# Dense expert tiles of a decoder trunk on one core: 64 early score chunks instead of 32, one copy for four tokens' gate products, gate steps given priority

## The chip, the core and the metric

The kernel runs on 1 core of one Trainium2 chip. The metric is the time of one execution on the device in microseconds (us). The engines are named as in the profile: PE is TensorE's matmuls, PEld its weight loads, DVE is VectorE, ACT is ScalarE, POOL is GpSimd, SP is SyncE, which here only issues transfers.

## What is computed

One layer of a decoder trunk, for a prompt of 1024 tokens and 32 sample tokens of width 1024. First come a modulation by a conditioning vector, one projection, three token mixers (a matrix memory, a gated unit, a pooling), an output projection and a layer norm. Then every token goes through a layer of 16384 small experts (PEER), and a second layer norm. The change concerns that expert layer. Cut to it:

```python
def peer(xm, w_pq, peer_keys, peer_u, peer_v):          # 8 heads, 128 keys, top 16
    q = jnp.einsum('nd,de->ne', x2, w_pq).reshape(n, PEER_HEADS, 2, PEER_DK)
    s = jnp.einsum('nhpd,hpkd->nhpk', q, peer_keys)
    s1, i1 = lax.top_k(s[:, :, 0], PEER_TOPK)
    s2, i2 = lax.top_k(s[:, :, 1], PEER_TOPK)
    cand = (s1[..., :, None] + s2[..., None, :])         # and cidx = i1 * 128 + i2
    top_s, top_pos = lax.top_k(cand, PEER_TOPK)
    idx = jnp.take_along_axis(cidx, top_pos, axis=-1)
    g = jax.nn.softmax(top_s, axis=-1)
    act = gelu(jnp.einsum('nd,nhkd->nhk', xk, peer_u[ik]))
    return jnp.einsum('nhk,nhkd->nd', gk * act, peer_v[ik])
```

So each token has 8 x 16 = 128 experts out of 16384, each with a row of `peer_u` and a row of `peer_v` (1024 numbers each).

## The kernel before

The prompt is cut into 8 tiles of 128 tokens; the 32 sample tokens are a ninth, small tile. The expert layer is done in two ways.

*Gathered tiles* (0, 1, 6, 7 and the small one): for each token slot one indirect transfer on GpSimd's queue fetches 128 rows of `peer_u` (0.524 MB), VectorE multiplies and sums them with the tokens; later 128 rows of `peer_v` come the same way and TensorE adds them up, two rows per four matmuls, into two PSUM banks (`acc`, L1354). Row buffers are few (6 of one kind and 6 of another), so a row is fetched when an older one has been used. There are 544 such steps for `peer_u` and 544 for `peer_v`; `g_gather` writes them, and gives their instructions a priority 2000 ahead of the place where they are written.

*Dense tiles* (2, 3, 4, 5, 512 tokens): all 16384 experts are computed for them, in 128 chunks of 128 experts. The score of a chunk (`scores`, L1067) is 24 matmuls of 128x128 by 128x512, since `peer_u` and the tokens are both split into a high and a low half-precision part; ScalarE and VectorE do the split of a loaded chunk of `peer_u`. The scores go through gelu, are multiplied by the gate of that token and expert (zero for the experts that are not chosen), split again, and four chunks at a time (a group) are multiplied with the split `peer_v` (`out`, L1174: 8 outputs of 12 matmuls for a group), whose sums VectorE adds up in SBUF (L1183). There are 32 groups. `g_dense` writes them; for each output it also writes a part of the next group's scores.

*The gates* of a dense tile (`g_weights`): for a token, a 128x128 table with a gate at (i1, i2) is a product of two matrices of ones and gates, with the gate in a high and a low part. VectorE makes the two masks for 16 tokens at a time (`ab`, L1042 and L1043), multiplies one by the high part (L1044), and gets the low part by a product for tokens NL to 15 (L1045), while ScalarE does it for tokens 0 to NL - 1 (L1047). TensorE makes two matmuls for each token (`pgm`, L1054), ScalarE copies four tokens' tables out of PSUM in two halves (L1057), turning them so that the token is the innermost index, into two tiles `gs` of 64 columns by 32 tokens. Every 32 tokens the two tiles are stored to DRAM (`G_d`, L1061). The dense stage loads them by group (L1105).

*Early scores* (`g_pre`): the scores of the chunks in `PRE`, one in four, are made before the dense stage: `peer_u` is loaded (0.524 MB), split (L1084 on ScalarE, L1085 on VectorE), the scores are copied (L1089) and stored to DRAM (`sd_d`, 0.262 MB, L1090). In the dense stage such a chunk's scores are loaded instead of its `peer_u` (L1143).

The order: the parts are generators. `run` books for each step three costs in us (TensorE, VectorE, transfers), always takes the part whose planned time is least, and so sets the order in which instructions are written. A scheduler then puts them into each engine's fixed order by their priority, which is the place of writing, less `AHEAD` for the parts named there: the mixing, routing and recurrence parts have 1000, the gate steps none. The main part waits until all gates, all early scores, the routing (`g_route`, `g_choice`) and 96 rows of tile 1's second gather are written, closes the early buffers and begins the dense stage. The costs booked in the dense stage are, for an output, an early chunk and any other chunk:

```python
            if op[0] == "o":
                yield 2.58, 0.66, 0
            elif op[1] in PRE:
                yield 0, 2.9, 3.0
            else:
                yield 5.15, 1.77 + 2.2, 3.7
```

and for a gathered row `c = 0, 1.14, 1.46` (`peer_u`) or `c = 0.43, 0, 1.46` (`peer_v`).

Of the kernel before, what the change touches and what calls it, by code (L numbers as in the profile page):

```python
# [7 lines left out]
F32 = mybir.dt.float32  # L8
# [5 lines left out]
AF = mybir.ActivationFunctionType  # L14
# [3 lines left out]
P = 128  # L18
# [10 lines left out]
LOW = -3.0e38  # L29
BUFS = {"ws": 5, "x": 2, "s": 6, "h": 8, "w": 3, "t": 4, D: 1, D // 2: 2}  # L30
LAG = 4
AHEAD = {"g_mixed": 1000, "g_routed": 1000, "g_even": 1000, "g_odd": 1000}
SPLIT = 1
COND = "ada", 0
EARLY = "proj", "gate"
# [18 lines left out]
ND = len(DENSE) * P  # L54
TB = 32
BB = 16
NL = 6
PRE = [4 * g + 3 for g in range(32)]
GROUP = 4
SW, SU, SV, SG_, SC = 2.0 ** 8, 2.0 ** 8, 2.0 ** 6, 2.0 ** 12, 0.25  # L60
CANDS = [(j, 16 // (j + 1)) for j in range(16)]
# [17 lines left out]
def kernel(ctx: ExitStack, tc: tile.TileContext, A, O):  # L79
    nc = tc.nc  # L80
    mm, tr = nc.tensor.matmul, nc.tensor.transpose
    V, S = nc.vector, nc.scalar
# [25 lines left out]
    def run(*parts):  # L108
# [6 lines left out]
        while parts:  # L115
# [8 lines left out]
            now = p[0]  # L124
            ahead = AHEAD.get(p[2].__name__, 0)
            tc.cur_priority -= ahead
# [44 lines left out]
    G_d = dram.tile([ND // TB, P, P, TB], F32, name="G_d")  # L171
    qkvo_d = dram.tile([NT + 1, P, 4, 512], F32, name="qkvo_d")
    sd_d = dram.tile([max(len(PRE), 1), P, ND], F32, name="sd_d")
    xd_d = dram.tile([len(DENSE), P, 2, KD, P], F16, name="xd_d")
# [840 lines left out]
    def g_weights(i, t):  # L1015

        sc = cur["build"]
# [18 lines left out]
        for b in range(P // BB):  # L1036
            ab = sc.tile("ab", [P, 3, BB, P], F16, 2)
            pairs = lambda a: a.rearrange("p t (c e) -> p t c e", e=2)
            f = [fx[:, j, b * BB:b * BB + BB, :].unsqueeze(2).to_broadcast([P, BB, P // 2, 2]) for j in range(4)]
            one = iota16.rearrange("p (c e) -> p c e", e=2).unsqueeze(1).to_broadcast([P, BB, P // 2, 2])  # L1040
            eq = ab[:, 2]
            V.tensor_tensor(out=pairs(ab[:, 0]), in0=one, in1=f[0], op=ALU.is_equal)  # L1042
            V.tensor_tensor(out=pairs(eq), in0=one, in1=f[1], op=ALU.is_equal)  # L1043
            V.tensor_tensor(out=pairs(ab[:, 1]), in0=pairs(eq), in1=f[2], op=ALU.mult)  # L1044
            V.tensor_tensor(out=pairs(eq[:, NL:]), in0=pairs(eq[:, NL:]), in1=f[3][:, NL:], op=ALU.mult)  # L1045
            for j in range(NL):
                S.activation(eq[:, j], eq[:, j], AF.Copy, scale=fl[:, b * BB + j:b * BB + j + 1])  # L1047
            if b * BB % TB == 0:
                gs = [sc.tile("gs", [P, 64, TB], F32, 2) for _ in range(2)]
            for t4 in range(0, BB, 4):  # L1050
                pg = bank("pgm", (P, 4, P))
                for j in range(4):
                    for e in range(2):
                        mm(pg[:, j, :], lhsT=ab[:, 0, t4 + j, :], rhs=ab[:, 1 + e, t4 + j, :], start=(e == 0), stop=(e == 1))  # L1054
                t0 = b * BB % TB + t4
                for e in range(2):
                    S.activation(gs[e][:, :, t0:t0 + 4].rearrange("p c t -> p t c"), pg[:, :, 64 * e:64 * e + 64], AF.Copy)  # L1057
                yield 0.6, 1.1, 0.4 * MB
            if (b + 1) * BB % TB == 0:
                for e in range(2):  # L1060
                    nc.sync.dma_start(G_d[i * (P // TB) + b * BB // TB, :, 64 * e:64 * e + 64, :], gs[e])  # L1061

    def scores(ps, us, xd):
        m = 0
# [5 lines left out]
    def g_pre():  # L1070
# [7 lines left out]
        for i in range(len(DENSE)):  # L1078
            nc.sync.dma_start(xd[:, i], xd_d[i])
        for i, n in enumerate(PRE):  # L1080
            u = xslab("up", (P, KD, P))
# [12 lines left out]
    def g_dense(sc):  # L1094
# [11 lines left out]

        todo = [n for n in range(nch) if n not in PRE]

# [31 lines left out]
        def ld_s(n):  # L1140
            if n in PRE:
                PS[n] = sc.tile("act", [P, ND], F32, 3)
                nc.sync.dma_start(PS[n], sd_d[PRE.index(n)])  # L1143

# [5 lines left out]
        def coef(n):  # L1150
            ps = PS.pop(n)
            if n in PRE:
                t = ps
# [572 lines left out]
```

## Time and profile before

| what | value |
|---|---|
| median of 3 runs | 3282.22 us (3278.94 to 3289.62) |
| the profiled execution, its own time | 3289.84 us |
| its span in the profile | 3288.1 us |
| PE busy | 2763.4 us, 84% |
| DVE busy | 2205.8 us, 67% |
| POOL busy | 1320.7 us, 40% |
| ACT busy | 938.7 us, 29% |
| transfers | 964.86 MB, mean 293 GB/s |

An engine's busy time is the sum over its instructions; a busy PE is not PE at its peak, because matmuls overlap and their ends are modelled. The clock column of the views is the granted TensorE clock as a share of full speed. The DMA column is the mean busy share of the core's 16 DMA engines. A "releaser" behind an idle time is what the engine waited for last.

### The profile page before, as it was taken

What the parts mean: (1) busy time and instruction counts of PE and PEld (TensorE: products, weight loads), DVE (VectorE), ACT (ScalarE), POOL (GpSimd) and SP (SyncE); (2) the same over time, 40 slices, a digit from 0 to 9 for tenths busy, and PEclk for the clock granted to TensorE, in tenths of its full rate; (3) what the DMA queues carried; (4) which work ended last, traced back from release to release, by engine and by line L of the source; (5) the groups of instructions that cost most, each with busy time, mean ns of one, the idle gap of its engine ahead of it and who ended that gap; (6) DMA issues with size and microseconds to landing.
All of it is one profiled execution on the core that took longest, in us unless ns stands there. A gap on an engine that the chain in (4) does not pass through costs nothing.

```text
span 3288.1 us, 44890 instructions
## 1 busy us (share of the span) xinstructions
PE 2763.4 (84%) x16366; PEld 1415.8 (43%) x16366; DVE 2205.8 (67%) x5763; ACT 938.7 (29%) x1618; POOL 1320.7 (40%) x1096
## 2 busy tenths in 40 slices
PE   6888983587976798987657999999999999559996
PEld 3447942444654356753333443344333343004443
DVE  2443998767788657789985774877777775015557
ACT  3413243112011124324564322322222222003331
POOL 0000366535444530045754454655665553650000
PEclk8988996688978899999867999999999999559998
DMA  9753898889998984488999999999999998993442
GB/s 293 253 175 132 300 347 296 293 294 327 322 341 275 336 324 155 161 318 308 346 356 361 333 353 348 379 374 364 385 387 353 345 382 291 333 325 123 144 126 76
DMA packets 370577, 964.86 MB, mean 293 GB/s; under 512 B 36933, under 2 KB 114884, under 8 KB 366252
## 3 DMA queue, kind: packets, MB, share of 16 engines
q0 software_dynamic: 156672, 570.49, 47.7%
q1 hardware_dynamic: 213684, 391.51, 34.2%
q8 instruction: 128, 2.10, 0.3%
q14 instruction: 93, 0.76, 0.1%
HBM read 892.92 MB, written 69.02 MB: 293 GB/s over the span
## 4 chain that ended last, share of the span: by engine, by line
PE 48%; DMA 12%; DVE 9%; issue 7%; ACT 2%; POOL 1%; SPq 0%; POOLq 0%; DVEq 0%; ACTq 0%
PE po L1174 19%; PE psd L1067 16%; DMA row<-in_peer_v,iT 6%; PE acc L1354 6%; DMA row<-in_peer_u,ii 3%; PE py L809 2%; DVE row L1297 2%; PE pqr L881 2%; POOL row L1270 1%; DMA G_d<-gs 1%; ACT gs L1057 1%; DMA v<-in_peer_v 1%; DMA act<-sd_d 0%; PE pvp L280 0%; DMA wo<-in_w_o 0%
## 5 line engine op out<-in xcount | busy, mean ns | idle before, releaser
L1270 POOL DMA_INDIRECT row<-in_peer_u,ii x544 | 679.8, 1250 | 987.2 <-DVE ii L1293 312.5
L1270 POOL DMA_INDIRECT row<-in_peer_v,iT x544 | 638.7, 1174 | 608.9 <-PE acc L1354 369.1
L1297 DVE SCALAR_TENSOR_TENSOR row<-row,x2u 128x1024 f32<-128x1024 f32 x544 | 657.2, 1215 | 161.9 <-DMA row<-in_peer_u,ii 148.7
L1067 PE MATMUL psd<-xd,us 128*128 128x512 f16 x3072 | 712.6, 384 | 21.1 <-ACT us L1084 15.0
L1174 PE MATMUL po<-vs,coef 128*128 128x512 f16 x3072 | 701.3, 381 | 19.9 <-ACT vs L1137 11.7
L1354 PE MATMUL acc<-row,cexp 128*32 128x512 f32 x2176 | 362.3, 720 | 176.4 <-DMA row<-in_peer_v,iT 175.5
L1174 PEld LDWEIGHTS <-coef 128*128 128x128 f16 x3072 | 294.5, 98 | 437.5 <-issue 81.3
L1067 PEld LDWEIGHTS <-us 128*128 128x128 f16 x3072 | 298.1, 99 | 418.5 <-issue 56.6
L881 PE MATMUL pqr<-x2T,wpq 128*128 128x128 f32 (+1 forms) x2304 | 282.2, 282 | 2.0 <-DVE z L817 1.0
L881 PEld LDWEIGHTS pqr<-x2T,wpq 128*128 128x128 f32 x2304 | 274.7, 198 | 8.9 <-DVE CA L929 1.5
L1159 DVE SCALAR_TENSOR_TENSOR act<-act,scale,g 128x512 f32<-128x512 f32 x128 | 95.9, 750 | 232.9 <-ACT act L1157 230.6
L1157 ACT ACTIVATE act<-psd,scale 128x512 f32<-128x512 f32 x96 | 65.9, 687 | 597.6 <-PE psd L1067 597.6
L1183 DVE SCALAR_TENSOR_TENSOR acc<-po,scale,acc 128x512 f32<-128x512 f32 x248 | 183.2, 746 | 71.0 <-PE po L1174 70.5
L1354 PEld LDWEIGHTS acc<-row,cexp 128*32 128x32 f32 x2176 | 49.9, 116 | 354.6 <-DMA row<-in_peer_v,iT 240.7
L1138 DVE SCALAR_TENSOR_TENSOR vs<-v,vs 128x1024 f16<-128x1024 f32 x128 | 155.5, 1219 | 47.0 <-ACT vs L1137 46.9
L1137 ACT ACTIVATE vs<-v 128x1024 f16<-128x1024 f32 x128 | 133.6, 1051 | 136.0 <-PE po L1174 68.0
L809 PE MATMUL py<-wo,Y 128*128 128x512 f32 (+1 forms) x288 | 141.5, 641 | 18.2 <-DMA wo<-in_w_o 11.5
L1054 PE MATMUL pgm<-ab 128*128 128x128 f16 x1024 | 100.9, 256 | 66.2 <-DVE ab L1044 30.4
L1057 ACT ACTIVATE gs<-pgm 128x256 f32<-128x256 f32 x256 | 124.9, 641 | 68.3 <-PE pgm L1054 42.6
L280 PEld LDWEIGHTS <-w 128*128 128x128 f16 x2160 | 124.0, 100 | 22.6 <-issue 19.5
L1121 DVE SCALAR_TENSOR_TENSOR us<-u,us 128x1024 f16<-128x1024 f32 x96 | 117.4, 1223 | 19.9 <-ACT us L1120 19.9
L1054 PEld LDWEIGHTS <-ab 128*128 128x128 f16 x1024 | 83.2, 118 | 102.3 <-issue 55.4
(344 smaller groups left out, 2860.0 us busy)
## 6 DMA issues: line engine op xcount, KB each, us to landing
v<-in_peer_v SPq DMA_DIRECT2D x128, 512.0 KB
u<-in_peer_uT SPq DMA_DIRECT2D x96, 512.0 KB
wpq<-in_w_pq SPq DMA_DIRECT2D x64, 512.0 KB
G_d<-gs SPq DMA_DIRECT2D x32, 1024.0 KB
g<-G_d SPq DMA_DIRECT2D x32, 1024.0 KB
wada<-in_w_ada SPq DMA_DIRECT2D x48, 512.0 KB
wf<-in_w_in SPq DMA_DIRECT2D x44, 512.0 KB
wo<-in_w_o SPq DMA_DIRECT2D x32, 512.0 KB
```

Source lines behind the costliest of these rows:

```text
L809: mm(py[t, e][:ns[t]], lhsT=Y_[t][:, k + j, :ns[t]], rhs=w[:, j, :], start=(k + j == 0), stop=(k + j == KD - 1))
L881: mm(pq[:, i * P:i * P + ns[t]], lhsT=w[:, k, :], rhs=X2[t][:, k, :ns[t]], start=(k == 0), stop=(k == KD - 1))
L1054: mm(pg[:, j, :], lhsT=ab[:, 0, t4 + j, :], rhs=ab[:, 1 + e, t4 + j, :], start=(e == 0), stop=(e == 1))
L1057: S.activation(gs[e][:, :, t0:t0 + 4].rearrange("p c t -> p t c"), pg[:, :, 64 * e:64 * e + 64], AF.Copy)
L1067: mm(ps, lhsT=us[a][:, k, :], rhs=xd[:, :, b, k, :], start=(m == 0), stop=(m == 23))
L1137: S.activation(vs[:, 0], v, AF.Copy, scale=SV)
L1138: V.scalar_tensor_tensor(out=vs[:, 1], in0=v, scalar=SV, in1=vs[:, 0], op0=ALU.mult, op1=ALU.subtract)
L1174: mm(po, lhsT=d[:, a, i * P:(i + 1) * P], rhs=vs[:, b, c % 2, :], start=(m == 0), stop=(m == 3 * GROUP - 1))
L1183: V.scalar_tensor_tensor(out=a, in0=po, scalar=scale[:, 3:4], in1=a, op0=ALU.mult, op1=ALU.add)
L1270: nc.gpsimd.indirect_dma_start(out=s[:], out_offset=None, in_=A[table], in_offset=bass.IndirectOffsetOnAxis(ap=idx, axis=0))
L1297: V.scalar_tensor_tensor(out=s, in0=s, scalar=1.0, in1=x2, op0=ALU.mult, op1=ALU.mult, accum_out=sv[:, k:k + 1])
L1354: return mm(pv[e][g:g + 32, :], lhsT=l, rhs=s[:, e * 512:e * 512 + 512], start=(j == 0), stop=(j == nj - 1), skip_group_check=True)
```

## The change

Four edits. `PRE` names every second chunk instead of every fourth, so 64 chunks' scores are made early and 64 are left for the dense stage. `NL` goes from 6 to 3, so ScalarE scales 3 of 16 tokens and VectorE 13. The two tiles `gs` of 64 columns become one of 128, a single copy moves four tokens' tables, and the tile is stored in four parts. The gate steps are given the priority that mixing and routing have.

```diff
-AHEAD = {"g_mixed": 1000, "g_routed": 1000, "g_even": 1000, "g_odd": 1000}
+AHEAD = {"g_mixed": 1000, "g_routed": 1000, "g_even": 1000, "g_odd": 1000, "g_gates": 1000}
...
-NL = 6
-PRE = [4 * g + 3 for g in range(32)]
+NL = 3
+PRE = [2 * g + 1 for g in range(64)]
...
             if b * BB % TB == 0:
-                gs = [sc.tile("gs", [P, 64, TB], F32, 2) for _ in range(2)]
+                gs = sc.tile("gs", [P, P, TB], F32)
...
                 t0 = b * BB % TB + t4
-                for e in range(2):
-                    S.activation(gs[e][:, :, t0:t0 + 4].rearrange("p c t -> p t c"), pg[:, :, 64 * e:64 * e + 64], AF.Copy)
+                S.activation(gs[:, :, t0:t0 + 4].rearrange("p c t -> p t c"), pg, AF.Copy)
                 yield 0.6, 1.1, 0.4 * MB
             if (b + 1) * BB % TB == 0:
-                for e in range(2):
-                    nc.sync.dma_start(G_d[i * (P // TB) + b * BB // TB, :, 64 * e:64 * e + 64, :], gs[e])
+                for e in range(4):
+                    c = slice(32 * e, 32 * e + 32)
+                    nc.sync.dma_start(G_d[i * (P // TB) + b * BB // TB, :, c, :], gs[:, c, :])
```

## Rows read from the trace of the kernel before

**Rows 1.** The page: busy time of each engine, share of the span, instructions.
```profile
PE 2763.4 (84%) x16366; PEld 1415.8 (43%) x16366; DVE 2205.8 (67%) x5763; ACT 938.7 (29%) x1618; POOL 1320.7 (40%) x1096
```

**Rows 2.** Stretches: us, busy PE, PEld, DVE, ACT, POOL, clock, DMA share, GB/s.
```profile
1060.00:1243.00 183.00, 152.41 (x889) 83.75 (x888) 111.52 (x399) 40.73 (x88) 79.06 (x73) 0.92 0.88 318
1243.00:1390.00 147.00, 133.19 (x991) 101.82 (x990) 118.23 (x555) 58.79 (x115) 3.41 (x4) 0.95 0.43 147
1390.00:1600.00 210.00, 166.00 (x1064) 89.05 (x1064) 186.34 (x649) 82.00 (x158) 120.39 (x80) 0.93 0.89 321
1600.00:1765.00 165.00, 92.92 (x739) 61.05 (x738) 135.50 (x190) 109.53 (x268) 101.68 (x65) 0.65 0.94 352
1765.00:2200.00 435.00, 426.78 (x2116) 170.80 (x2115) 297.19 (x430) 123.34 (x157) 225.87 (x189) 0.99 0.98 357
2200.00:2500.00 300.00, 291.21 (x1432) 116.97 (x1430) 221.69 (x323) 78.77 (x102) 174.29 (x148) 0.99 1.01 377
2500.00:2790.00 290.00, 287.11 (x1439) 114.06 (x1442) 199.25 (x292) 82.45 (x107) 139.94 (x120) 1.00 0.96 344
2790.00:2958.00 168.00, 99.27 (x437) 12.01 (x429) 19.07 (x40) 3.93 (x6) 98.04 (x102) 0.57 0.92 326
2958.00:3288.00 330.00, 303.78 (x1392) 135.87 (x1392) 200.03 (x304) 93.03 (x116) 0.00 (x0) 0.96 0.37 117
```

**Rows 3.** Score matmuls (L1067), one stretch: us, PE, PEld, clock, DMA share, GB/s.
```profile
2958.00:3288.00 330.00, 122.89 (x552) 54.02 (x552) 0.96 0.37 117
```

**Rows 4.** The chain that ended last, after 2958: start us, us, what.
```profile
2967.42 5.18 PE psd L1067 x24
```

**Rows 5.** GpSimd's groups, 1765 to 2790 and then 1243 to 1390, with idle time before.
```profile
L1270 POOL DMA_INDIRECT row<-in_peer_v,iT x253 | 301.0, 1190 | 316.3 <-PE acc L1354 221.7 <-issue 42.0 <-DVE row L1297 33.3
L1270 POOL DMA_INDIRECT row<-in_peer_u,ii x202 | 239.0, 1183 | 164.2 <-DVE row L1297 101.4 <-issue 41.3 <-PE acc L1354 13.5
...
L1270 POOL DMA_INDIRECT row<-in_peer_u,ii x2 | 1.9, 938 | 143.3 <-PE ps L886 143.0 <-issue 0.3
```

**Rows 6.** TensorE's timeline, 1590 to 1800, then the chain, 1600 to 1800.
```profile
1693.91 2.72 PE L1054 MATMUL pgm<-ab 128*128 128x128 f16 x24 [8.09 <-ACT gs L1057]
...
1682.22 10.96 DMA G_d<-gs
```

**Rows 7.** Gate matmuls (L1054) by stretch, columns as in rows 3.
```profile
1390.00:1610.00 220.00, 22.63 (x286) 18.48 (x287) 0.94 0.89 319
1610.00:1765.00 155.00, 63.07 (x561) 52.77 (x560) 0.63 0.95 357
```

**Rows 8.** VectorE's groups by form, 1060 to 1765.
```profile
L1044 DVE TENSOR_TENSOR ab<-ab,fx 128x2048 f16<-128x2048 f16 x32 | 38.8, 1214 | 0.1
L1085 DVE SCALAR_TENSOR_TENSOR us<-up,us 128x1024 f16<-128x1024 f32 x32 | 38.7, 1210 | 11.6 <-ACT us L1084 11.6
...
L1045 DVE TENSOR_TENSOR ab<-ab,fx 128x1280 f16<-128x1280 f16 x32 | 25.8, 812 | 0.1
```

**Rows 9.** ScalarE's groups by form, whole span.
```profile
L1057 ACT ACTIVATE gs<-pgm 128x256 f32<-128x256 f32 x256 | 124.9, 641 | 68.3 <-PE pgm L1054 42.6 <-DMA G_d<-gs 25.6
...
L1047 ACT ACTIVATE ab<-ab,fl 128x128 f16<-128x128 f16 x192 | 59.2, 388 | 68.1 <-DVE ab L1044 66.2 <-issue 1.9
...
L1084 ACT ACTIVATE us<-up 128x1024 f16<-128x1024 f32 x32 | 33.6, 1050 | 0.0
...
L892 ACT ACTIVATE scores<-ps 128x256 f32<-128x256 f32 x64 | 21.4, 382 | 54.3 <-PE ps L886 36.6 <-DVE TI L900 9.1 <-issue 5.8
L1089 ACT ACTIVATE so<-psd 128x512 f32<-128x512 f32 x32 | 19.1, 597 | 71.0 <-PE psd L1067 71.0
```

**Rows 10.** Transfers of 1390 to 2958, then of 2958 to 3288.
```profile
DMA packets 209627, 548.82 MB, mean 350 GB/s; under 512 B 16768, under 2 KB 70144, under 8 KB 205946
...
DMA packets 25647, 38.61 MB, mean 117 GB/s; under 512 B 1152, under 2 KB 13440, under 8 KB 25632
```

## Prediction, made before the changed kernel was run

> **What bounds the kernel now.** I read the page's head first: of 3288.1 us TensorE is busy 84%, VectorE 67%, and only 45% or less of the others [rows 1]. That average hides five stages, so the second view is the table of stretches [rows 2]. From 1060 to 1765 us (routing, gate products, early scores, gathers) TensorE is busy 152.4 + 133.2 + 166.0 + 92.9 = 544.5 of 705 us, and in the last 165 us the granted clock is 0.65. From 1765 to 2790 it is busy all the time at a clock of 0.99 to 1.00, while the DMA engines are at 0.96 to 1.01: two limits at once. From 2790 to 2958 only gathered rows are left to work on. From 2958 to 3288 there is dense work alone: TensorE full, DMA at 0.37.
>
> The third view is the score line in the last stretch [rows 3]: 552 matmuls there, 23 of the dense stage's 96 chunks; the other 73 stand before 2790. The chain gives 5.18 us for a chunk's 24 [rows 4]; output matmuls have the same shape. The fourth view is what GpSimd waits for in the dense stage: 221.7 + 13.5 us for TensorE and 33.3 + 101.4 us for VectorE to give row buffers back [rows 5]. So the rows are paced by the place their consumers have in the engines' fixed orders, and the order on TensorE matters as much as any rate. Last, the end of the early stage, where the gate products are made after the early scores: TensorE waits 8.09 us for ScalarE's copies, and the chain runs 10.96 us through a store of gate products for which ScalarE waited [rows 6]. The dense stage waits for just that.
>
> **Gate steps ahead.** Nothing is added, only the order. 561 of 1024 gate matmuls (512 tokens, two each) stand after 1610 [rows 7]. If they go earlier, the stretch to 1765 is left to scores. It lies on VectorE: 3 x 1.214 + 0.812 = 4.45 us per 16 tokens [rows 8], 32 times, 143 us in all, wherever it stands. What they can be put ahead of is the routing of the last group, for which GpSimd waits 143.0 us [rows 5]; VectorE has 147 - 118.2 = 29 us free there [rows 2], TensorE 14. I price that at nothing; bound: the roughly ten blocks that could move ahead of it, 45 us, less 29 free, so +16 us on the gathers.
>
> **NL from 6 to 3.** ScalarE loses 96 scalings of 0.388 us, 37 us. VectorE's product grows from 1280 to 1664 elements: between 0.812 (1280) and 1.214 (2048) [rows 8] that is 1.01 us, +6.4 us over 32.
>
> **One copy for four tokens.** 256 copies of 256 elements at 0.641 us, 164 us, become 128 of 512. This copy's output is strided: another copy of 256 elements out of PSUM takes 0.382, one of 512 takes 0.597 [rows 9]. So 0.597 + (0.641 - 0.382) x 2 = 1.115 us, 143 us in all: ScalarE gains 21 us (bounds: 88 at 0.597, nothing at twice 0.641). The tile now is one of the same size as the two, so a block of 32 tokens waits for all its stores, not for the first of two: 1.05 MB more (128 x 64 x 32 numbers), 2.9 us at 357 GB/s, up to 15 times, 44 us of waiting on ScalarE. Behind it queue the score splits and copies; ScalarE is busy 291 of 705 us [rows 2], and this cover hides both signs. The 32 more store issues on SP cost nothing: it only issues, and all its transfers are asked for well ahead. If gates stay last, 44 us is the price.
>
> **32 more early chunks, before the dense stage.** TensorE: 32 x 5.18 = 166 us. ScalarE: 32 x (1.050 + 0.597) = 53 us; with the two gains it ends lower than before. VectorE: 32 x 1.21 = 39 us [rows 8, 9], in all 552 + 39 + 6 = 597 us. TensorE decides: 544.5 + 165.8 = 710 us of work. The fullest stretch, 1243 to 1390, is busy 133.19 of 147, 90.6% [rows 2]; at that fill it takes 784 us, and dense starts at 1844, +79. Bounds: +5 at 100%, +215 at the present 77%. In my favour, and left out of the sum: at the 0.63 clock 561 gate matmuls took 63.07 us against 22.63 for 286 at 0.94 [rows 7], some 19 us that scores beside them would give back.
>
> Traffic: 32 loads of 0.524 MB move here and 32 stores of 0.262 MB are new, 25.2 MB. Their issues stand in SP's queue, where dense loads come behind them; GpSimd issues the rows from its own. From 1390 to 1765 the stretches moved 210 x 321 + 165 x 352 = 125.5 MB. To 1844, at the mean of 350 GB/s that 1390 to 2958 shows [rows 10], 158.9 MB fit: less 125.5 and 25.2 that leaves 8.2 MB, 16 rows of 0.524 MB that the later stages need not gather. Of the 102 rows in the 168 us after 2790 [rows 2] these are -26 us.
>
> **The dense stage.** Before 2790 a third of 73 chunks, 24.3, no longer need scores: 126 us of TensorE. But the stretch moved 435 x 357 + 300 x 377 + 290 x 344 = 368 MB; 24.3 loads of 0.262 in place of 0.524 MB leave 362 MB. At 377 GB/s, the best stretch, that is 960 us: the gain is 65 us, not 126. The tail after 2958 loses 7.7 chunks, -40 us.
>
> The rate is the doubtful term: the same stretch moved its 368 MB at a mean of 359 GB/s, and at that it would gain 17 us only (rival 2). The 377 over 300 us at 1.01 of the engines [rows 2] shows that the engines can give it where enough is asked for, so I keep 377. The Trainium skill ("DMA: Bandwidth & Descriptors", Specifications) gives about 358 GB/s as one core's share of HBM, a rule that speaks against this change, whose gain hangs on transfers; by it the 362 MB take 1011 us and the sum below comes to 3287 instead of 3236. By that rule, the trace disagrees: 300 us at 377.
>
> **Sum with the order as it is**: 3288 + 79 - 26 - 65 - 40 = 3236.
>
> **The order moves.** The kernel's plan books for four chunks 36.1 us of TensorE and 14.1 of DMA now, 30.9 and 13.4 then, and 1.46 of DMA per row; between them 15.1 rows fit now, 12.0 then, 0.795 of it. Traced are 253 + 202 = 455 rows [rows 5] beside 23 of the 32 groups (the tail of 330 us being 9 of 36). That is 19.8 a group; at 0.795 of it, 15.7, the 455 less the 16 saved stand beside 28 groups, five more. Each carries 2.10 (v) + 1.05 (u) + 0.52 (scores) + 1.05 (gates) = 4.72 MB, five 23.6 MB, 63 us at 377 GB/s, and takes 31 us off the tail, 155: net -92 us, 3144. The fixed order comes from priorities as well as from this plan, so I take three quarters, -69: 3167. The profiled execution is 3289.8 us for a span of 3288.1, and 7.6 above the median of 3282.2: 3167 + 1.7 - 7.6 = 3161. I forecast **3160 us**, 3.7% less.
>
> **Rivals.** (1) *More comes*: TensorE is full to 1770 (+5) and the order moves wholly. 3144 - 74 = 3070, in place of which the 16 rows are not saved, +26: 3096, so 3090. For it: all bytes from 1390 on, 548.8 + 38.6 [rows 10] and 16.8 new ones, 604 MB, take 1602 us at 377 GB/s, to 2992. Against it: at 350 they take 1726 us, to 3116, and no stretch on TensorE that has routing in it passes 91%.
>
> (2) *Order stays*: consumers keep their places beside the dense groups. At 377 GB/s the sum says 3236, 3230 by the median. At the stretch's own 359 it gains 17 in place of 65: 3284, 3278, no change. For it: GpSimd's waits are on buffers, not on DMA, and a mean of 359 is what 1025 us have now. Against the low rate: 2500 to 2790, at 344, is the least of the three, so the mean is not a ceiling. The Trainium skill's share of about 358 (the page above) would end there too; the trace's 377 is against it.
>
> (3) *Slower, the added traffic is paid in full at the old mean*: the order of (2), and early scores push the rows back before 1844 as well, where they now run at 321. To the last row 548.8 + 25.2 - 6.4 = 568 MB at 350 GB/s are 1622 us from 1390, to 3012, and 290 us of tail: 3302, 3296 by the median, +0.4%. It decides from 353 GB/s downward (568 MB at 353 and 290 us of tail are 1898 us, no change). For it: 350 is the mean of 1390 to 2958. Against it: in the first 210 of these us at 321 and the last 168 at 326 the rows waited for others, and early scores fill the first of these.
>
> **Numbers.** Under 0.3% (10 us) this kernel's runs, 3278.9 to 3289.6, cannot be told from no change. Forecast, order mostly moved (3110 to 3220): 0.42. Rival 1, below that: 0.20. Rival 2 at the high rate (3220 to 3265): 0.10; at the low one (3265 to 3292): 0.10, of which 0.02 lie more than 0.3% below 3282. Rival 3, above: 0.18. Faster 0.42 + 0.20 + 0.10 + 0.02 = 0.74, same 0.08, slower 0.18. The range of 3060 to 3295 leaves out most of rival 3 and a little below; the likeliest case's own is 3110 to 3220.
>
> **What would show it.** Right: gate matmuls thin after 1620 and the granted clock there above 0.9; dense outputs from 1800 to 1890; DMA at 1.0 with TensorE below 0.97 in the dense stage; the tail without rows under 250 us. Wrong: a wait of GpSimd much over 143 us for routing; gate copies still the last thing before the dense stage; a tail of 290 us; rows that stop alone for over 168 us because TensorE ran through the dense groups too early.

## The result: 0.7% faster where 3.7% was forecast

The changed kernel takes 3274.53 us (median of 20 runs, 3252.89 to 3287.9), the kernel before 3291.77 on the same chip: a ratio of 0.9933, 95% interval 0.9913 to 0.9953. The profiled execution has a span of 3266.5 us. In the page TensorE has the same 16366 matmuls in 44 us less [rows 1]; ScalarE has 192 instructions less, but is busy only 4 us less.

```profile
PE 2719.2 (83%) x16366; PEld 1402.8 (43%) x16366; DVE 2214.2 (68%) x5763; ACT 934.7 (29%) x1426; POOL 1337.3 (41%) x1096
```

Stretches of the kernel after, in the columns of [rows 2], cut where its own stages end (dense outputs from 1998, the last row at 3011):

```profile
1060.00:1243.00 183.00, 155.95 (x900) 86.60 (x902) 107.98 (x388) 38.54 (x72) 74.53 (x71) 0.92 0.87 316
1243.00:1390.00 147.00, 126.57 (x939) 96.35 (x932) 115.78 (x532) 55.22 (x83) 1.40 (x2) 0.93 0.40 142
1390.00:1600.00 210.00, 160.65 (x1041) 89.69 (x1039) 176.96 (x615) 70.13 (x103) 116.22 (x79) 0.90 0.86 310
1600.00:1765.00 165.00, 133.83 (x787) 61.14 (x788) 119.58 (x204) 66.31 (x92) 93.56 (x66) 0.92 0.92 340
1765.00:1850.00 85.00, 70.05 (x426) 31.49 (x425) 53.48 (x76) 34.10 (x45) 45.49 (x36) 0.98 0.95 361
1850.00:1998.00 148.00, 86.00 (x557) 41.31 (x556) 78.89 (x101) 58.78 (x81) 70.54 (x57) 0.77 0.98 368
1998.00:2200.00 202.00, 202.00 (x1015) 79.59 (x1014) 137.91 (x203) 60.04 (x79) 93.22 (x81) 0.99 0.93 338
2200.00:2500.00 300.00, 265.99 (x1311) 106.68 (x1309) 224.62 (x330) 76.88 (x98) 197.53 (x161) 0.94 1.04 393
2500.00:2790.00 290.00, 269.36 (x1356) 105.10 (x1355) 201.60 (x302) 81.49 (x106) 154.86 (x134) 0.96 0.99 368
2790.00:3011.00 221.00, 212.99 (x1124) 75.91 (x1126) 111.24 (x153) 59.56 (x78) 98.92 (x92) 0.99 0.96 341
3011.00:3266.00 255.00, 228.70 (x1044) 101.66 (x1036) 165.69 (x267) 66.83 (x88) 0.00 (x0) 0.94 0.37 117
```

Read the row from 1850 first: the stage before the dense one goes on to 1998, where [rows 2] show the dense stage from 1765 on, and in its last 148 us TensorE is busy for 86 and its granted clock is 0.77, part at 2.4 and part at 1.2 GHz. Then the last two: gathered rows are used up to 3011, and of the 1124 matmuls beside the last of them 388 are the rows' own (L1354); in the 2790 to 2958 of [rows 2], where 102 rows stood alone, 424 of 437 were. Behind the last row there are 255 us, not 330. What stands in them, output and then score matmuls of the kernel after, and the output matmuls of before (its 552 score matmuls are [rows 3]):

```profile
3011.00:3266.00 255.00, 158.65 (x720) 70.60 (x720) 0.94 0.37 117
...
3011.00:3266.00 255.00, 69.47 (x312) 30.53 (x312) 0.94 0.37 117
```
```profile
2958.00:3288.00 330.00, 183.61 (x828) 81.16 (x828) 0.96 0.37 117
```

A group has 96 output matmuls. So 7.5 groups stand behind the last row, 8.6 before, and 13 chunks' scores, 23 before. The next rows are GpSimd's groups in the dense stage, as far as rows and dense groups stand side by side, and then the output matmuls of the same stretch. Before:

```profile
L1270 POOL DMA_INDIRECT row<-in_peer_v,iT x249 | 294.1, 1181 | 313.3 <-PE acc L1354 220.6 <-issue 41.6 <-DVE row L1297 31.7
L1270 POOL DMA_INDIRECT row<-in_peer_u,ii x198 | 234.5, 1185 | 156.8 <-DVE row L1297 95.8 <-issue 39.5 <-PE acc L1354 13.5
```
```profile
1787.00:2790.00 1003.00, 514.58 (x2232) 212.03 (x2230) 0.99 0.98 359
```

and after:

```profile
L1270 POOL DMA_INDIRECT row<-in_peer_v,iT x306 | 352.9, 1153 | 376.3 <-PE acc L1354 286.8 <-issue 64.5 <-DMA row<-in_peer_u,ii 8.2
L1270 POOL DMA_INDIRECT row<-in_peer_u,ii x160 | 191.6, 1197 | 97.8 <-DVE row L1297 37.7 <-issue 29.7 <-DMA row<-in_peer_v,iT 10.5
```
```profile
1998.00:3011.00 1013.00, 542.67 (x2352) 222.28 (x2350) 0.97 0.99 364
```

Before, 447 rows beside 2232 / 96 = 23.25 groups: 19.2 rows a group, 43.1 us. After, 466 rows beside 24.5 groups: 19.0 a group, 41.3 us. **The ledger of the span**: dense start +211 (1786.7 to 1997.8), the stretch of rows and groups +10 (1.25 groups more, 52 us, less 1.8 us on each of 23.25, 42), the rows alone -168, the work behind the last row -75. Together -22, and the spans differ by 21.6. Two large terms, 243 us of gain and 221 of loss, nearly cancel.

### The profile page after: what moved, and what is told of

Same layout as the page of the kernel before. It is cut to its first block, busy times and chain, and to the rows that moved or that the text cites. A ratio compares the mean times of both kernels' runs of the same rounds, so it can differ in the third digit from the quotient of the medians.

```text
span 3266.5 us, 44808 instructions
## 1 busy us (share of the span) xinstructions
PE 2719.2 (83%) x16366; PEld 1402.8 (43%) x16366; DVE 2214.2 (68%) x5763; ACT 934.7 (29%) x1426; POOL 1337.3 (41%) x1096
## 5 line engine op out<-in xcount | busy, mean ns | idle before, releaser
L1270 POOL DMA_INDIRECT row<-in_peer_u,ii x544 | 696.4, 1280 | 975.8 <-DVE ii L1293 316.9
L1067 PE MATMUL psd<-xd,us 128*128 128x512 f16 x3072 | 742.5, 392 | 81.5 <-ACT us L1084 76.3
L1174 PE MATMUL po<-vs,coef 128*128 128x512 f16 x3072 | 701.5, 381 | 68.9 <-ACT vs L1137 50.3
L1067 PEld LDWEIGHTS <-us 128*128 128x128 f16 x3072 | 303.5, 101 | 502.0 <-ACT us L1084 110.6
L1174 PEld LDWEIGHTS <-coef 128*128 128x128 f16 x3072 | 293.0, 98 | 498.6 <-issue 129.4
L1354 PE MATMUL acc<-row,cexp 128*32 128x512 f32 x2176 | 317.5, 639 | 115.7 <-DMA row<-in_peer_v,iT 115.6
L1157 ACT ACTIVATE act<-psd,scale 128x512 f32<-128x512 f32 x64 | 44.0, 687 | 462.7 <-PE psd L1067 462.7
L1354 PEld LDWEIGHTS acc<-row,cexp 128*32 128x32 f32 x2176 | 49.7, 110 | 247.1 <-DMA row<-in_peer_v,iT 134.8
L1056 ACT ACTIVATE gs<-pgm 128x512 f32<-128x512 f32 x128 | 127.1, 1079 | 94.7 <-PE pgm L1054 65.2
L1164 ACT ACTIVATE coef<-act 128x512 f16<-128x512 f32 x128 | 79.7, 624 | 190.8 <-DVE act L1159 190.6
L1085 DVE SCALAR_TENSOR_TENSOR us<-up,us 128x1024 f16<-128x1024 f32 x64 | 77.9, 1217 | 62.4 <-ACT us L1084 62.3
L1054 PE MATMUL pgm<-ab 128*128 128x128 f16 x1024 | 84.1, 238 | 27.9 <-DVE ab L1044 10.8
```

What stands on the lines that cost most here:

```text
L1056: S.activation(gs[:, :, t0:t0 + 4].rearrange("p c t -> p t c"), pg, AF.Copy)
L1067: mm(ps, lhsT=us[a][:, k, :], rhs=xd[:, :, b, k, :], start=(m == 0), stop=(m == 23))
L1174: mm(po, lhsT=d[:, a, i * P:(i + 1) * P], rhs=vs[:, b, c % 2, :], start=(m == 0), stop=(m == 3 * GROUP - 1))
L1270: nc.gpsimd.indirect_dma_start(out=s[:], out_offset=None, in_=A[table], in_offset=bass.IndirectOffsetOnAxis(ap=idx, axis=0))
L1354: return mm(pv[e][g:g + 32, :], lhsT=l, rhs=s[:, e * 512:e * 512 + 512], start=(j == 0), stop=(j == nj - 1), skip_group_check=True)
```

## What was tried

Every kernel below is told by the same three marks of its profiled execution: the first dense output (L1174), the last gathered row (the start of the last matmul that uses one, L1354), and what of the span follows it. Times are medians of all runs, ratios are to the kernel before, run beside each (its medians there: 3289.65 to 3296.73).

| kernel | early chunks | time | ratio, 95% interval | dense from | last row | behind it |
|---|---|---|---|---|---|---|
| before | 32 | 3291.77 | 1 | 1787 | 2959 | 329 |
| after | 64 | 3274.53 | 0.9933 [0.9913, 0.9953] | 1998 | 3011 | 255 |
| e1 | 64 | 3285.31 | 0.9968 [0.9953, 0.9984] | 2006 | 3033 | 253 |
| e2 | 32 | 3333.26 | 1.0115 [1.0089, 1.0141] | 1818 | 2996 | 329 |
| e3 | 64 | 3262.47 | 0.9901 [0.9879, 0.9923] | 1969 | 3007 | 252 |
| e4 | 64 | 3245.5 | 0.985 [0.9826, 0.9873] | 1953 | 2991 | 254 |
| e5 | 64 | 3250.3 | 0.9877 [0.9855, 0.9899] | 1971 | 2994 | 253 |
| e6 | 64 | 3226.29 | 0.9799 [0.9779, 0.9819] | 1858 | 2970 | 255 |
| e7 | 32 | 3313.98 | 1.0057 [1.0036, 1.0078] | 1816 | 2986 | 328 |
| e8 | 64 | 3287.03 | 0.9979 [0.9961, 0.9997] | 1996 | 3038 | 254 |
| e9 | 32 | 3316.18 | 1.0065 [1.0047, 1.0082] | 1809 | 2977 | 329 |
| e10 | 64 | 3271.49 | 0.9935 [0.9912, 0.9958] | 2007 | 3030 | 254 |
| e11 | 64 | 3325.36 | 1.0098 [1.0072, 1.0125] | 2006 | 3134 | 185 |
| e12 | 32 | 3194.57 | 0.9687 [0.9662, 0.9712] | 1796 | 3031 | 164 |
| e13 | 32 | 3213.0 | 0.9766 [0.974, 0.9792] | 1797 | 3031 | 166 |
| e14 | 32 | 3226.55 | 0.9799 [0.977, 0.9828] | 1823 | 3067 | 156 |
| e15 | 64 | 3263.76 | 0.9918 [0.9891, 0.9946] | 2009 | 3026 | 247 |
| e16 | 64 | 3224.6 | 0.9791 [0.9763, 0.9819] | 1953 | 3000 | 222 |
| e17 | 42 | 3201.58 | 0.9704 [0.969, 0.9718] | 1851 | 3055 | 145 |
| e18 | 16 | 3283.23 | 0.9956 [0.994, 0.9972] | 1802 | 3058 | 226 |

**The parts alone (e1, e2, e3, e7).** e1 is the kernel before with the new `PRE` alone, e2 the changed kernel with the old one.

```diff
-PRE = [4 * g + 3 for g in range(32)]
+PRE = [2 * g + 1 for g in range(64)]      # e1; e2 the other way round
```

> The kernel before with 64 early chunks and nothing else of the change. In the trace of the changed kernel the first dense output stands at 1998 us instead of 1787 (+211), and from there to the end it takes 1269 us instead of 1501 (-232). Theory A (the 32 chunks alone make both numbers, because the early stage is no better filled than before): first dense output 1960 to 2040, ratio to before 0.985 to 1.005. Rival (the gate edits hold the stage short, and without them 64 chunks cost more): first dense output after 2040, slower than before by over 1%.

> The changed kernel with 32 early chunks: NL 3, one copy, four stores, gate steps ahead. Theory A: the gate steps fill nothing by themselves; the dense stage starts 0 to 30 us earlier, ratio to before 0.990 to 1.003. Rival (gates are what the dense stage waits for, and going ahead frees it): first dense output 50 to 100 us earlier than 1787, ratio 0.965 to 0.985. Rival (one tile for the gate products makes each block wait for all its stores): 15 to 45 us later, ratio 1.005 to 1.014.

e3 is the changed kernel, and e7 is e2, without the priority of the gate steps:

```diff
-..., "g_odd": 1000, "g_gates": 1000}
+..., "g_odd": 1000}
```

> The changed kernel with the gate steps' priority taken back, all else kept. Theory A: no matter; within 10 us of the changed kernel (ratio to before 0.989 to 0.998), gate steps in the same places. Rival (priority is what moved the gate steps among the early chunks): gate matmuls thicken after the last early chunk again, first dense output 20 to 60 us later, ratio 1.000 to 1.012.

> The kernel before with NL 3, one copy and four stores, 32 early chunks, gate steps without priority. All three with the priority cost 1.15%. Theory D (the priority costs it: GpSimd's wait for routing grew from 143 to 149 us and gate steps stand in front of others): ratio 0.990 to 1.003. Rival (the one tile that waits for all four stores costs it): ratio 1.006 to 1.015 here as well.

The chunks alone give both large terms (dense from 2006, 253 us behind the last row); the gate edits alone give neither. Of these kernels the three marks go by the number of early chunks, and that part of the change is where its time is decided. The small ratios don't add up, though: e1 -0.3%, e2 +1.2%, both together -0.7%. e2 and e7 start the dense stage 31 and 29 us later than the kernel before, as the case with one tile for the gate products had it; but ScalarE's waits for the stores are 27.0 us in e2 and 47.4 in e7 (25.6 before), so these waits explain at most the second, and e9 below starts 22 us later with no gate edit at all.

**How far an order moves by itself (e9, e10).** Any edit lets the scheduler write another order. So the plan's cost of an early chunk was changed by 0.1 us, which changes no instruction, in the kernel before (e9) and in the changed one (e10):

```diff
-            yield 5.15, 1.1, 0.75 * MB
+            yield 5.05, 1.1, 0.75 * MB
```

> The kernel before, doing the same work with the same priorities; only the plan's cost of an early chunk is 5.05 us instead of 5.15, so the fixed orders are dealt anew (3309 places of TensorE's order differ). Theory E (the order dealt matters by as much as the edits: the kernel before has a good deal, its last row at 2959 against 2986 and 2996 in the two other kernels with 32 early chunks): last row 2965 to 3000, tail 329, ratio 1.002 to 1.013. Rival (the order is no matter, gate edits cost what was measured): ratio 0.997 to 1.003.

> The changed kernel with the same neutral edit (5.05 for 5.15 in the plan). Theory E: tail 254, last row anywhere in 2990 to 3038 as in the five kernels with 64 chunks, ratio to before 0.983 to 1.000. Rival (order no matter): ratio 0.991 to 0.996.

The kernel before loses 0.65%, its last row going from 2959 to 2977; the changed kernel keeps its ratio. With 32 chunks and the plan's weights as they were, the last row stands at 2959, 2977, 2986 and 2996 in four orders: the kernel before has the best of them. Effects of some 0.6% that any one edit shows here can't be told from this, those of the gate edits among them; nor can the 0.3% by which e3 is faster than the changed kernel. Against its own other order, e9, the change is worth 0.9933 / 1.0065, 1.3%.

**What the dense start and the rows wait for (e4, e5, e6, e8).** Groups of the changed kernel in the page, then its timeline from 1702 us on (start, us, engine, line):

```profile
L1067 PE MATMUL psd<-xd,us 128*128 128x512 f16 x3072 | 742.5, 392 | 81.5 <-ACT us L1084 76.3
```
```profile
1702.34 0.60 ACT L1089 ACTIVATE so<-psd 128x512 f32<-128x512 f32 x1 [0.66 <-PE psd L1067]
1702.84 1.05 ACT L1084 ACTIVATE us<-up 128x1024 f16<-128x1024 f32 x1
...
1703.94 0.39 PE L1067 MATMUL psd<-xd,us 128*128 128x512 f16 x1 [0.64 <-ACT us L1084]
...
1711.82 0.39 PE L1067 MATMUL psd<-xd,us 128*128 128x512 f16 x1 [0.64 <-ACT us L1084]
```

ScalarE's order has the copy of one chunk's scores ahead of the split of the next, so TensorE, done with a chunk, waits for both: 76.3 us in all, though only 0.64 of the 7.9 us from one chunk to the next here, the rest of which is matmuls of scores, gates and rows. e4 moves the copy to VectorE, and e8 is e4 without the gate steps' priority:

```diff
-            S.activation(o, ps.rearrange("p i t -> p (i t)"), AF.Copy)
+            V.tensor_copy(o, ps.rearrange("p i t -> p (i t)"))
```

> The changed kernel with the copy of early scores out of PSUM on VectorE, not on ScalarE. In the changed kernel ScalarE's fixed order puts each chunk's split behind the copy of the scores before it, so TensorE waits (76 us in all) and chunks come every 7.9 us or more instead of 6.5. Theory B (that order is what leaves TensorE unfilled): TensorE's wait for the split falls below 30 us, the first dense output comes 40 to 80 us before 1998, ratio to before 0.970 to 0.985. Rival (transfers fill the stage: 25 MB more at 340 to 368 GB/s): first dense output within 15 us of 1998, the wait only changes its name, ratio 0.990 to 0.998. Rival (the gate steps come last anyway): last gate copy still at 1940 to 1960.

> The changed kernel with the score copy on VectorE and the gate steps' priority taken back: the two changes that gained, together. If they add up: 0.985 less the 0.003 that the priority cost, ratio to before 0.978 to 0.985, last row 5 to 15 us before the 2991 of the copy alone. If transfers bound it already (359 GB/s with the copy alone): no gain over 0.985.

With the priority (e4 against the changed kernel) TensorE's wait for the split falls from 76.3 to 25.1 us, the dense stage starts 45 us earlier, and the time is 0.8% less. Without it (e8 against e3) the wait falls from 45.8 to 37.0, but the dense stage starts 27 us later, and the time is 0.8% more. The wait is real, but what it is worth isn't settled: these orders differ by more than it.

e5 loads `peer_u` for every second early chunk only, and uses it twice, so half of the early scores are those of the neighbour; e6 makes an early chunk of the high parts alone, 8 matmuls in place of 24, so its scores lack the low parts.

```diff
-            u = xslab("up", (P, KD, P))
-            nc.sync.dma_start(u, A["peer_uT"][n])
+            if i % 2 == 0:
+                u = xslab("up", (P, KD, P))
+                nc.sync.dma_start(u, A["peer_uT"][n])
```
```diff
-            scores(ps, us, xd)
+            for k in range(KD):
+                mm(ps, lhsT=us[0][:, k, :], rhs=xd[:, :, 0, k, :], start=(k == 0), stop=(k == KD - 1))
```

> The changed kernel, but peer_u is loaded only for every second early chunk and split and used twice (so half of the early scores are those of the chunk before): 32 loads, 16.8 MB, are gone, all matmuls, splits, copies and stores stay. In the four 64-chunk and 32-chunk traces so far 1390 to 2950 us carries 350 to 359 GB/s whatever the kernel, and the run ends some 254 us after the last gathered row. Theory C (transfers set when the gathered rows end): 16.8 MB at 355 GB/s are 47 us, last row 35 to 55 us before the changed kernel's 3011, ratio to before 0.975 to 0.984. Rival (engine orders pace the rows, transfers only follow): last row within 15 us of 3011, mean rate falls to about 345 GB/s, ratio 0.989 to 0.996.

> The changed kernel with 8 of the 24 matmuls of each early chunk (the high parts only), all loads, splits, copies and stores kept: 64 x 16 x 0.2158 = 221 us of TensorE leave the early stage. Theory C (transfers set the end of the rows): the dense stage may start earlier, but the last row moves by under 25 us and the ratio to before stays above 0.983. Rival (TensorE's unfilled early stage, which the forecast was built on): first dense output 100 us or more before 1998, last row 50 us or more earlier, ratio 0.955 to 0.978.

16.8 MB less, worth 47 us at 354 GB/s, bring the last row 17 us forward, no more than the 18 and 19 us by which the neutral edits of e9 and e10 moved it: that transfers alone set the rows' end is not borne out. 64 x 16 matmuls less, 221 us at 5.18 us for 24, bring the dense start 140 us forward, two thirds of the +211, but the last row only 42.

e6 says two things more. Its early chunks are 512 matmuls, those of the kernel before 768, and yet its dense stage starts 71 us later than that kernel's, and 40 later than that of e2, which has the same gate edits and the same 768. So a part of an early chunk's price is not TensorE's own time; TensorE's line for these chunks, from 1390 to 1858, has a wait of 98.1 us for ScalarE's split:

```profile
L1088 PE MATMUL psd<-xd,us 128*128 128x512 f16 x376 | 121.5, 456 | 98.1 <-ACT us L1084 98.1
```

And what the earlier start gains doesn't reach the last row. 533 rows are left for e6's dense stage, 466 for the changed kernel's, but behind the last row stand the same 720 output and 312 score matmuls. The same 24.5 groups come before it, and then the last 78 rows stand alone, as in the kernel before (columns of [rows 2]):

```profile
2835.00:2970.00 135.00, 76.22 (x338) 8.72 (x336) 18.84 (x38) 4.01 (x7) 76.08 (x78) 0.55 0.93 326
```

**The gap with rows alone (e11, e12, e13, e15, e16).** In [rows 2] the order of the kernel before leaves its last 102 rows without dense work beside them. The planner's weight of the rows in the dense stage decides how early they are written. e12 is the kernel before with one number changed, e11 the changed kernel with 1.2:

```diff
-    ("dense", {"g_gather": 0.8}),
+    ("dense", {"g_gather": 1.0}),             # e12; 1.2 in e11
```

> The changed kernel with the weight of gathered rows in the plan's dense phase 1.2 instead of 0.8: the same work, but in TensorE's fixed order only 489 output and 192 score matmuls stand behind the last row, not 720 and 312, so the tail should be 170 us instead of 255. Theory F (my forecast's step: if dense groups move beside the rows, the tail's time is gained less their transfers): last row 20 to 50 us later than 3011, ratio to before 0.975 to 0.988. Rival (rows and dense groups share transfers and TensorE so fully that the last row moves by what the tail loses, 85 us): ratio 0.989 to 0.997.

> The kernel before with that weight 1.0 instead of 0.8: 384 output and 216 score matmuls behind the last row instead of 828 and 552, a tail of about 145 us instead of 329. In the trace of before TensorE idles 69 of 168 us beside the last 102 rows, which this fills. Theory F: last row 60 to 120 us later than 2959, ratio 0.965 to 0.985, so that this edit alone gives as much as the change. Rival: last row 185 us later, ratio 0.997 to 1.003.

Two stretches of e12, in the columns of [rows 2], and the output matmuls of its stretch from 2790 to the last row:

```profile
2790.00:2958.00 168.00, 166.11 (x880) 58.95 (x879) 69.87 (x87) 42.32 (x54) 79.73 (x76) 1.00 0.93 334
2958.00:3031.00 73.00, 69.87 (x357) 24.17 (x359) 38.67 (x61) 19.00 (x25) 31.70 (x27) 0.98 0.89 314
```
```profile
2790.00:3031.00 241.00, 106.10 (x456) 42.50 (x456) 0.99 0.92 328
```

To 2790 its rows are those of before. Then 456 / 96 = 4.75 groups run beside the last 102 rows, the last of which comes 72 us later, and 164 us are left behind them instead of 329: -3.1%, over four times what the change gives. In e11, which has no such gap, the same means bring the last row 123 us later, more than the 85 of its rival case, and 70 us off the end: slower. Its order has the groups too early instead: from 2790 to 3011 TensorE is full, while transfers fall to 232 GB/s and 57 rows are fetched:

```profile
2790.00:3011.00 221.00, 221.00 (x937) 75.36 (x935) 90.33 (x114) 50.89 (x68) 58.41 (x57) 1.00 0.70 232
```

Whether e12 was one lucky order, and whether the early chunks add to it, were the next four: e13 is e12 with the 0.1 us of e9, e15 the changed kernel with 1.0, e14 and e16 are e12 and e15 with the score copy on VectorE (the diffs are those above).

> The kernel before with the plan's weight of the rows in the dense stage at 1.0 instead of 0.8, and the plan's cost of an early chunk at 5.05 instead of 5.15, which changes nothing but the order that the scheduler writes. Behind its last row the order has 397 output and 216 score matmuls (384 and 216 without the second edit). If the gap in which the kernel before waits for its last 102 rows is what the weight took away: tail 160 to 170, last row 3010 to 3050, 3170 to 3215. If the gain of that weight was the luck of one order: the last row after 3060 or a tail over 200, and 3240 or more.

> The kernel before with weight 1.0, and each early chunk's score copy on VectorE instead of ScalarE. 360 output and 206 score matmuls behind the last row. If ScalarE's order of score copy and split delays the early chunks with 32 of them as with 64: dense start some 20 earlier than 1796, tail 155 to 165, 3160 to 3195. If it counts only where 64 chunks make the stage before the dense one long: as with weight 1.0 alone, 3185 to 3215.

> The changed kernel with weight 1.0. Behind its last row the order has 696 output and 290 score matmuls, 720 and 312 without the edit: there is little left to move. If the early chunks gain only by filling the hole that the rows leave in the dense stage: last row 3010 to 3035, tail 245 to 250, 3255 to 3285, so slower by over 2% than the kernel before with weight 1.0 (3194.57). If the early chunks' saving is additional to the refilled hole: 3120 to 3170.

> The changed kernel with the score copy on VectorE and weight 1.0. 607 output and 264 score matmuls behind the last row. If the weight only trades a later last row for a shorter tail once there is no hole: last row 3010 to 3030, tail 215 to 230, 3230 to 3260, the same as without the weight (3245.5). If the early chunks' saving adds to the refilled hole: under 3180.

e13 has the marks of e12 and 0.9766: the gain is not the luck of one order, though its size, 2.3 or 3.1%, hangs on the order. e15 is the case without addition: last row 3026, 247 us behind it, 3263.76 us. At the same weight the changed kernel is slower than the kernel before by 1.6 to 2.4% (0.9918 against 0.9766 and 0.9687); 64 early chunks without the gate edits were not run at it. e14 missed: the score copy on VectorE starts the dense stage 27 us later instead of 20 earlier. e16 is better than its filling case, 3224.6, with the earlier last row of e4 and 222 us behind it, and far from additional. Moving the copy helped in e4 and e16 and hurt in e8 and e14, so no more is said of it.

**What an early chunk costs (e17, e18).** e12 with 42 and with 16 early chunks:

```diff
-PRE = [4 * g + 3 for g in range(32)]
+PRE = [g for g in range(3, 128, 3)][:42]      # e17; [8 * g + 7 for g in range(16)] in e18
```

> The kernel before with weight 1.0 and 42 early chunks (every third) in place of 32. 350 output and 168 score matmuls behind the last row, 384 and 216 with 32. If early chunks take off the end only what stands behind the last row, and push the dense start by what they cost before it (211 us for 32 of them): dense start 1796 + 20 to 70, last row 3030 to 3060, tail 145 to 155, 3180 to 3215, the same as with 32. If each chunk's saving of scores reaches the end: 10 x 5.18 us less, under 3165.

> The kernel before with weight 1.0 and 16 early chunks. 521 output and 360 score matmuls behind the last row. If the stage before the dense one has no room for early chunks, as the dense start 211 us later with 64 suggests: dense start 1680 to 1720, last row 2960 to 3000, tail 210 to 220, 3175 to 3215, the same as with 32. If that stage has room for the first 32, and only the next 32 push the dense start: dense start 1770 to 1796, last row 3020 to 3040, 3235 to 3260.

The dense stage starts at 1802, 1796, 1851 and 2009 with 16, 32, 42 and 64 early chunks. Up to 32 they are free: in e18 TensorE's same stretches, in the columns of [rows 2], were emptier (112.0 and 72.8 us of TensorE, 166.0 and 92.9 in [rows 2]) where 32 chunks filled them without moving the end.

```profile
1390.00:1600.00 210.00, 112.03 (x888) 77.20 (x886) 170.02 (x570) 79.94 (x192) 107.55 (x75) 0.69 0.76 267
1600.00:1765.00 165.00, 72.77 (x550) 44.12 (x554) 125.71 (x266) 79.75 (x198) 112.14 (x63) 0.61 0.80 289
```

The next 10 cost 55 us, the 22 after them 157: 5.5 and 7.2 us each, for 5.18 of TensorE's work. Both prices are rough: one order of each kernel was run, and a neutral edit moved the dense start by 22 us (e9). The 2009 is that of e15, which has the gate edits; e1, without them and at the old weight, has 2006. 42 take 18 us off the end but bring the last row 24 later (against e12), and its time is that of 32 within what an order moves. 16 leave 226 us at the end. e18's expectation missed in both its cases: the dense start is that of free chunks, but the last row, 3058, and the time are some 20 us above it; why isn't known.

## Why the prediction was wrong, by its steps

**The gate steps ahead (priced 0).** The gate matmuls (L1054) after, in the columns of [rows 7]:

```profile
1390.00:1610.00 220.00, 19.08 (x232) 16.57 (x232) 0.90 0.85 307
1610.00:1765.00 155.00, 18.88 (x232) 17.27 (x232) 0.92 0.94 346
1765.00:1980.00 215.00, 31.84 (x376) 27.90 (x376) 0.88 0.96 365
```

Of 1610 to 1765 both signs came: 232 in place of 561, and the granted clock at 0.92, which was 0.63. But it was not the priority that brought them. e1 and e3, with 64 chunks and without it, have 215 and 240 gate matmuls there at 0.92 and 0.97; e2, with it and 32 chunks, has 513 at 0.65. The score matmuls of the added chunks fill that stretch (404, which were 10). Nor did the gates get done early; they spread over the longer stage, and the wrong sign came too: the last gate copy, at 1955.8, is the last of the stage, as the chain shows.

```profile
1928.89 2.74 ACT gs L1056 x3
1932.51 1.55 SPq L1061
1934.10 15.46 DMA G_d<-gs
1950.80 2.74 PE pgm L1054 x24
1953.55 10.51 PE psd L1067 x48
...
1966.85 29.44 DMA g<-G_d
1997.84 1.89 PE po L1174 x4
```

The copies wait for a store, and the dense stage for a load of gates of 29.44 us, among transfers that keep the engines at 0.98: 42 us lie between the last gate copy and the first output, 24 before (1763.0 to 1786.7). The wait for routing from 1243 on, feared at 16 us more, is 147.3 (143.0 in [rows 5]):

```profile
L1270 POOL DMA_INDIRECT row<-in_peer_u,ii x1 | 0.9, 936 | 147.3 <-PE pgm L1054 147.3
```

**NL, and one copy.** The prices of one instruction held: 1.01 us estimated, 1014 ns measured; 1.115 us estimated, 1079 measured. The gains of ScalarE did not. The forecast took counts times durations, but instructions that follow each other on ScalarE overlap, and [rows 9] have 124.9 us of busy time for the 256 copies, not 164. The 128 new ones are busy 127.1, so the gain is -2 us and not 21. The scalings fall from 59.2 to 31.4 us, 28 and not 37. ScalarE's waits for the stores of gates, feared at 44 us more, are 25.3 us (25.6 in [rows 9]).

```profile
L1056 ACT ACTIVATE gs<-pgm 128x512 f32<-128x512 f32 x128 | 127.1, 1079 | 94.7 <-PE pgm L1054 65.2 <-DMA G_d<-gs 25.3 <-issue 3.9
```
```profile
L1047 ACT ACTIVATE ab<-ab,fl 128x128 f16<-128x128 f16 x96 | 31.4, 390 | 74.2 <-DVE ab L1044 74.1
```
```profile
L1045 DVE TENSOR_TENSOR ab<-ab,fx 128x1664 f16<-128x1664 f16 x32 | 32.3, 1014 | 0.2
```

ScalarE's timeline, ten copies in a row before and eight after, gives 0.46 us for one of 256 and 0.90 for one of 512:

```profile
1739.28 4.56 ACT L1057 ACTIVATE gs<-pgm 128x256 f32<-128x256 f32 x10
```
```profile
1949.71 7.17 ACT L1056 ACTIVATE gs<-pgm 128x512 f32<-128x512 f32 x8 [8.24 <-DMA G_d<-gs]
```

**The dense start, +79: the first step that failed.** It took the fullest stretch, 90.6%, as the fill that the stage would reach. The stage from 1060 to 1998 has 155.95 + 126.57 + 160.65 + 133.83 + 70.05 + 86.00 = 733 us of TensorE in 938, 78%; the 77% that stood as the bound (+215) was the answer, +211. e17 and e18 show what the fill hid: 32 chunks had already taken the room. From there a chunk's 5.18 us over such a fill, 6.6 us, lies between the 5.5 and 7.2 that were measured; that this is all of the price is not shown, and e6 speaks against it. Of TensorE's 205 us without work there 160 stand before the matmuls of early scores, of rows and of gates, for the split, the rows, and the masks and gate copies:

```profile
L1067 PE MATMUL psd<-xd,us 128*128 128x512 f16 x1584 | 387.7, 393 | 81.5 <-ACT us L1084 76.3 <-DVE us L1085 4.4 <-issue 0.7
...
L1354 PE MATMUL acc<-row,cexp 128*32 128x512 f32 x610 | 97.2, 659 | 50.3 <-DMA row<-in_peer_v,iT 50.3
L1054 PE MATMUL pgm<-ab 128*128 128x128 f16 x1024 | 84.1, 238 | 27.9 <-DVE ab L1044 10.8 <-DVE ab L1045 9.1 <-ACT gs L1056 7.4
```

The first of these grows with the chunks: it was 15.0 us before.

**Sixteen rows saved, -26.** The sum took these rows off twice, here from the 102 that stand alone, and in the step on the order from the 455 beside the groups. The longer stage took more than sixteen: 447 + 102 rows were left for the dense stage before, 466 after, 83 fewer. That is the -168 of the ledger, the rows alone being gone, but it is bought with 211 us of later start.

**Dense stretch, -65 at 377 GB/s.** A group takes 41.3 us after, at 364 GB/s; 43.1 before, at 359. Over the 23.25 groups that stood there that is 42 us, between the 17 of the mean rate and the 65 of the best stretch. The rate of 393 in 2200 to 2500 was had for 300 us, and not kept: 368 follows, then 341. To the last row from 1390 on:

```profile
DMA packets 227793, 574.70 MB, mean 355 GB/s; under 512 B 18481, under 2 KB 74033, under 8 KB 227694
```

The Trainium skill ("DMA: Bandwidth & Descriptors", Specifications), with its share of about 358 GB/s for one core, is close to all such means here (343 to 359 from 1390 to the last row with 32 or 64 early chunks, weight 0.8). By that figure as a limit the trace disagrees: 393 over 300 us.

**The order moves, five groups: the step that failed by most.** The plan's booked costs were read as the mix that the order would have: 15.7 rows a group in place of 19.8, so 28 groups beside the rows. The traces show 19.2 before and 19.0 after, and before the last row 24.5 groups in place of 23.4 (the 3072 output matmuls less the 828 behind it, by 96). So 1.1 groups left the tail, not five. With the ten chunks' scores, 10 x 5.18 = 52 us, that is the -75 us. It is the order as written that fixes this number, and not how many rows are left: all eight kernels with 64 early chunks and the old weight have 720 output and 312 score matmuls behind the last row, with 466 to 533 rows left at the dense start, and all four with 32 have 828 and 552, with 544 to 549 left. What failed is the step from booked costs to that order: the 28 groups were worked out from a ratio of costs, and were not read from an order. Why the plan ends the rows at 24.5 groups and not elsewhere stays open. e12 shows that it can move them: at the weight 1.0, with 548 rows left, 2688 / 96 = 28 groups stand before the last row, 19.6 rows each, and the gap is gone.

**The rivals.** Rival 2 had the low rate and the unmoved order, and its 3265 to 3292 holds the result; but it kept the start at +79 and the tail near 290, so the number came by errors that cancel. Rival 3 named the place of the last row, 3012 (568 MB at 350), and it came at 3011.2 (574.7 MB at 355); to be right within a microsecond is luck, as six kernels that do this work (64 chunks, the old weight) have it from 2991 to 3038. The tail it gave, 290, was 35 us too long.

What stays open besides: what sets the 37 to 47 us between the last rows of orders with the same chunks and weight, what ScalarE's order of copy and split is worth, and what the part of an early chunk's price is that isn't TensorE's time.

## What to carry to other kernels

Work that is moved into an earlier stage is free only as long as that stage has idle time which it can use; try the stage with less of that work (16 chunks here), since if its end doesn't move there is room, and past that point price the work at no less than its own time over the stage's fill as it is on average, not as it is at its best. When the end is work that stands behind the last transfer of a fixed order, first look for a stretch where transfers run alone: closing it by the planner's one weight brought 2.3 to 3.1%, and moving work to shorten the end 0.7%. When an instruction's duration is multiplied by a count, set the product beside the busy time of the group: where it is larger, the instructions overlap. Before reading an effect under one per cent, change a number that changes no instruction and see what the order alone does.

## What the runs showed of the chip that was not expected

One core's transfers ran at 393 GB/s over 300 us with the DMA engines at 1.04, though the same kernel's mean from 1390 to its last row is 355. ScalarE's copy into a strided tile costs 1079 ns for 512 elements, 641 for 256 [rows 9], while a copy of 512 with a plain output took 597: 0.48 us less; each further element costs 1.7 ns in the one and 0.84 in the other (0.382 for 256). These are durations; in a row the strided copies overlap, and take 0.90 and 0.46 us each. An order written anew from the same instructions moved the time by up to 0.8% (e12 and e13), more than the 0.2 to 0.3% to which these ratios are known.
